# Gate biases, ln1's vectors and the residual x loaded on GpSimd's queue, and ten low weight parts made by adding DMAs

## The chip, the cores and the metric

The kernel runs on one core of a Trainium2 chip. The metric is the time of one execution on the device in microseconds (us). The engines are TensorE (PE in the profile), VectorE (DVE), ScalarE (ACT), GpSimd (POOL) and SyncE (SP). SP does no arithmetic here, it issues DMAs; GpSimd does arithmetic and issues DMAs from its own queue. Each engine, and each queue of DMA issues, takes its instructions strictly in order: one that waits holds up all behind it.

## The reference

One layer of an encoder on 512 tokens of 1024 channels, in float32. Only the parts that matter here:

```python
mod = silu(c) @ w_ada + b_ada                       # 6 vectors of 1024: shift, scale, gate for both halves
h = normalize(x) * (1 + sc_m) + sh_m
q, k, v, u, g_sb, g_ssm = split(h @ w_in)           # token mixer
y_sb  = stick_breaking_attention(q, k, v) @ w_sb_up # 8 heads of 64
y_ssm = s5_branch(u, ..., w_glu, b_glu) @ w_ssm_up
y = (sigmoid(g_sb) * y_sb + sigmoid(g_ssm) * y_ssm) @ w_out
x = layer_norm(ALPHA * x + (1 + g_m) * y, ln1_g, ln1_b)
h = normalize(x) * (1 + sc_f) + sh_f
gate, up = split(h @ w_ffn_in)                      # channel mixer, 2816 hidden
y = (silu(gate) * up) @ w_ffn_out
x = layer_norm(ALPHA * x + (1 + g_f) * y, ln2_g, ln2_b)
```

## The kernel before

Every float32 product is made of three products of a rounded type: operands are split into a high part (a cast) and a low part (the value less its high part), and `mm3` adds high by high, high by low and low by high. So each weight tile, 128 partitions of 1024 values (512 KB, `raw`), is loaded by SP, cast to `whi` on ScalarE, and its low part `wlo` is made in one of two ways: by a subtraction on VectorE or GpSimd (`sub`), or by a copy with factor -1 on ScalarE and a DMA from GpSimd's queue that adds `raw` to it (the adding DMA, L181; `unit` with no engine given). There are 8 buffers for `raw` (the w_ada tiles, `ra`, use the same ones) and 4 each for `whi` and `wlo`. All other tiles of 128 x 512 lie in 53 slots (`s`), given out first in, first out.

The stages in order of time: the normalisation and the S5 branch with the projections q, k, v (to 155 us); attention over four pairs of heads (155 to 324 us), between whose steps the products of 16 gate tiles (g_sb, g_ssm) stand; the glu and the up-projections (to 389 us); w_out in two halves of two token blocks, `proj` (389 to 440 us); the layer norm `ln1_block` for four token blocks (412 to 478 us); the channel mixer (478 to 808 us), and the last layer norm (to 823 us).

After each of the gate tiles 9 to 15, `later` puts a piece of the work on w_ada. The first four are `ada_gate`: GpSimd clears the tile (L257), a row of b_ada is loaded into its first partition by SP, two w_ada tiles are loaded by SP, and VectorE adds their 8 slices up, each times a value of c (L252). The tile that is cleared is a slot that an earlier product must have released.

The order of each engine's instructions is worked out ahead of time by a scheduler with streams of priorities ("feed" for weights, "attn", "gates", "later", "mix", "ffn"), from its own estimates of durations. Only SP's loads (`load`, L146) keep the order in which the program is written. ln1's gain and shift (`bcast`, four loads) stand in front of the glu weights in that order; the residual x of a token block is loaded in `proj` ahead of that half's w_out tiles, and GpSimd scales one half of it (L921).

In the channel mixer the first two pairs of column tiles (`first`) are two tiles through `unit` and two through `slot_unit`; FENG gives GpSimd the low parts of three and VectorE that of one. Both are needed when ln1's output h of two token blocks is there (`first_half(0)`). Behind it stand the products `p_x1` and `p_b` of further column pairs (dp = 0, 1 first), whose low parts VectorE makes in `operand`, then `first_half(256)`.

## Time and profile before

| | |
|---|---|
| median of 3 runs | 826.23 us (822.55 to 826.59) |
| the profiled execution | 824.6 us, its span 822.9 us |
| TensorE busy | 758.1 us (92%) |
| VectorE busy | 586.4 us (71%) |
| ScalarE busy | 438.8 us (53%) |
| GpSimd busy | 148.4 us (18%) |
| TensorE's mean granted clock | 0.968 of full speed |

A busy share is an average over stages. In 153 to 244, 340 to 440 and 520 to 804 us TensorE has no gap; its idle time lies in the first 60 us, in 244 to 331 us, in 440 to 478 us and at the end. In the profile the name of a buffer has no number: `s` is any slot, `b` a PSUM bank.

### The profile page before, as it was taken

How to read it: one execution, taken by the hardware profiler on the slowest of the kernel's cores; microseconds unless marked ns; L12 is line 12 of the kernel's file. 1: busy time of each engine (PE TensorE's matmuls, PEld its weight loads, DVE VectorE, ACT ScalarE, POOL GpSimd, SP SyncE). 2: the span in 40 equal slices, each digit the busy share in tenths (PEclk: the TensorE clock that was granted, in tenths of full speed). 3: DMA queues.
4: the chain of work that ended last, by engine and by line, in shares of the span. 5: the costliest groups of instructions: out<-in, count | busy, mean ns of one | idle time of the engine just before them, and what ended most of it. 6: DMA issues, size and time to landing. Idle time of an engine off the chain costs nothing.

```text
span 822.9 us, 12321 instructions
## 1 busy us (share of the span) xinstructions
PE 758.1 (92%) x4767; PEld 667.5 (81%) x4767; DVE 586.4 (71%) x975; ACT 438.8 (53%) x715; POOL 148.4 (18%) x161
## 2 busy tenths in 40 slices
PE   4989989999996797999994999999999999999995
PEld 2878879988885676787883989999999999888884
DVE  5798474884658774878799898777787876434267
ACT  4375644678987676761435473534445456532211
POOL 1443244512323221001634000000000000000013
PEclk9999998999997999899998899999999999999998
DMA  9992227964207792925941004414445344440001
GB/s 281 361 242 67 52 64 153 237 137 77 52 10 196 228 232 92 350 70 187 358 120 52 1 19 136 155 53 146 144 143 183 104 139 145 157 148 27 1 26 76
DMA packets 99498, 111.49 MB, mean 135 GB/s; under 512 B 4456, under 2 KB 86384, under 8 KB 99440
## 3 DMA queue, kind: packets, MB, share of 16 engines
q1 hardware_dynamic: 95552, 96.82, 37.1%
...
q14 instruction: 21, 0.17, 0.1%
...
## 4 chain that ended last, share of the span: by engine, by line
PE 75%; DVE 10%; DMA 6%; issue 3%; ACT 2%; SPq 2%; POOL 1%; POOLq 0%; DVEq 0%; ACTq 0%
PE b L149 74%; DMA ra<-w_ada 3%; SPq L146 2%; DMA s<-w_in 1%; DVE s L252 1%; DVE st L288 1%; DMA raw<-w_glu 1%; DMA wlo<-raw 1%; DVE h L159 1%; DVE s L407 1%; DMA s<-x 0%; DVE s L159 0%; DVE s L972 0%; DVE s L943 0%; DVE s L477 0%
## 5 line engine op out<-in xcount | busy, mean ns | idle before, releaser
L149 PE MATMUL b<-h,whi 128*128 128x256 f32 (+1 forms) x896 | 216.5, 331 | 20.8 <-DVE h L159 9.4
L149 PEld LDWEIGHTS b<-h,whi 128*128 128x128 f32 x896 | 151.5, 191 | 36.5 <-DVE h L159 9.6
L159 DVE TENSOR_TENSOR wlo<-raw,whi 128x1024 fp32r<-128x1024 f32 x103 | 129.6, 1264 | 72.1 <-ACT whi L178 37.1
L149 PE MATMUL b<-s,whi 128*128 128x256 f32 (+1 forms) x800 | 168.5, 308 | 7.6 <-ACT whi L178 6.8
L149 PE MATMUL b<-h,wlo 128*128 128x256 f32 (+1 forms) x448 | 148.2, 331 | 1.4 <-DMA wlo<-raw 1.4
L149 PEld LDWEIGHTS b<-s,whi 128*128 128x128 f32 x800 | 129.7, 190 | 18.0 <-ACT whi L178 6.9
L149 PE MATMUL b<-whi,s 128*128 128x512 f32 (+1 forms) x392 | 122.6, 390 | 0.0
L149 PE MATMUL b<-s,wlo 128*128 128x256 f32 (+1 forms) x400 | 121.5, 306 | 0.0
L159 DVE TENSOR_TENSOR s<-s,s 128x512 fp32r<-128x512 f32 (+4 forms) x112 | 76.4, 689 | 56.4 <-PE b L149 23.0
L178 ACT CAST whi<-raw 128x1024 fp32r<-128x1024 f32 x66 | 69.0, 1048 | 84.7 <-PE b L149 66.5
L1054 ACT CAST whi<-raw 128x1024 fp32r<-128x1024 f32 x70 | 72.7, 1050 | 77.5 <-PE b L149 41.6
L149 PEld LDWEIGHTS b<-h,wlo 128*128 128x128 f32 x448 | 85.8, 192 | 8.9 <-DMA wlo<-raw 1.9
L149 PEld LDWEIGHTS b<-whi,s 128*128 128x128 f32 x392 | 73.2, 188 | 16.6
L149 PE MATMUL b<-s,s 128*128 128x128 f32 (+2 forms) x438 | 81.9, 317 | 2.0 <-POOL s L159 1.4
L164 ACT CAST s<-s 128x512 fp32r<-128x512 f32 (+1 forms) x106 | 57.7, 569 | 41.3 <-DMA s<-w_in 12.1
L149 PEld LDWEIGHTS b<-s,wlo 128*128 128x128 f32 x400 | 75.7, 190 | 3.7
L149 PEld LDWEIGHTS b<-s,s 128*128 128x128 f32 x438 | 68.5, 192 | 11.2 <-POOL s L159 1.6
L149 PE MATMUL b<-wlo,s 128*128 128x512 f32 (+1 forms) x196 | 76.4, 390 | 0.0
L1233 POOL TENSOR_TENSOR s<-s,s 128x512 f32<-128x512 f32 x6 | 8.5, 1430 | 357.1 <-DVE s L1232 357.1
L159 POOL TENSOR_TENSOR s<-s,s 128x512 fp32r<-128x512 f32 (+1 forms) x32 | 40.2, 1264 | 79.0 <-ACT s L164 77.6
L1047 DVE TENSOR_TENSOR raw<-raw,raw 128x1024 f32<-128x1024 f32 x40 | 48.6, 1219 | 4.8 <-DMA raw<-w_ffn_in 4.3
L252 DVE SCALAR_TENSOR_TENSOR s<-ra,ca,s 128x256 f32<-128x256 f32 x88 | 47.2, 557 | 4.0 <-DMA ra<-w_ada 3.2
...
## 6 DMA issues: line engine op xcount, KB each, us to landing
...
```

Source lines behind the costliest of these rows:

```text
L146: return tc.keep_in_program_order(nc.sync.dma_start(out=o, in_=i))
L149: return nc.tensor.matmul(o, lhsT, rhs, start=start, stop=stop, skip_group_check=True, **kw)
L159: return eng.tensor_tensor(dst, a, b, ALU.subtract)
L164: acopy(h[:, :n], x[:, :n])
L178: acopy(hi, raw)
L252: stt(dst, r_, ca[:, k:k + 1], init if k == 0 else dst, ALU.mult, ALU.add)
L288: V.bn_stats(st[:, i, :], x)
L407: e.scalar_tensor_tensor(p_, n, -c, p_, ALU.mult, ALU.add)
L1047: tt(r, x, y, ALU.add)
L1054: acopy(hi, x)
L1233: G.tensor_tensor(z[h], z[h], l2b[h], ALU.add)
```

## The change

A new helper, `aside`, issues a load on GpSimd's queue, in whatever place the scheduler gives it. It takes the loads of the b_ada rows (eight), of ln1's and ln2's vectors (four each) and of the residual x (eight of 256 KB). In `proj` the x loads, and GpSimd's scaling of one half, are written behind the w_out tiles instead of ahead of them. A new helper, `lower`, makes a low part; with no engine given it does so by ScalarE's copy and an adding DMA. With it the four tiles of `first` (FENG is gone) and the operands of `p_x1` and `p_b` for dp = 0 and 1 get their low parts by ten adding DMAs (two of 128 x 1024 and four of 128 x 512, then four of 128 x 1024). In the changed file the lines move: L149 becomes L153, L159 becomes L163, L181 becomes L169, L257 becomes L264; `aside` is L150.

```diff
@@ -57,7 +57,7 @@
 PL = 5
 TAIL = 256
 
-ENG, FENG = "VGVVVGVGGGGVVGGG", "GGGV"
+ENG = "VGVVVGVGGGGVVGGG"
 
 
 XE, BE, ME, HE = "VVVV", "VVVV", "VVAVAAAV", "VVVVVVVV"
@@ -145,6 +145,10 @@
     def load(o, i):
         return tc.keep_in_program_order(nc.sync.dma_start(out=o, in_=i))
 
+    def aside(o, i):
+
+        return G.dma_start(out=o, in_=i)
+
     def mm(o, lhsT, rhs, start, stop, **kw):
         return nc.tensor.matmul(o, lhsT, rhs, start=start, stop=stop, skip_group_check=True, **kw)
 
@@ -158,17 +162,24 @@
     def sub(dst, a, b, eng=V):
         return eng.tensor_tensor(dst, a, b, ALU.subtract)
 
+    def lower(l, x, h, eng):
+
+        if eng is None:
+            act(l, x, AF.Copy, scale=-1.0)
+            G.dma_start(out=l, in_=x, accum_op=ALU.add)
+        else:
+            sub(l, x, h, eng)
+
     def split(x, n=512, eng=V, keep=False):
 
         h, l = get(F32R), get(F32R)
         acopy(h[:, :n], x[:, :n])
-        sub(l[:, :n], x[:, :n], h[:, :n], eng)
+        lower(l[:, :n], x[:, :n], h[:, :n], eng)
         if not keep:
             put(x)
         return h, l
 
     def unit(view, a, b, eng=V):
-
 
         with prio("feed"):
             raw = wp.tile([P, D], F32, tag="raw", name=nm("raw"), bufs=NRAW)
@@ -176,11 +187,7 @@
             hi = wp.tile([P, D], F32R, tag="whi", name=nm("whi"), bufs=NHI)
             lo = wp.tile([P, D], F32R, tag="wlo", name=nm("wlo"), bufs=NHI)
             acopy(hi, raw)
-            if eng is None:
-                act(lo, raw, AF.Copy, scale=-1.0)
-                G.dma_start(out=lo, in_=raw, accum_op=ALU.add)
-            else:
-                sub(lo, raw, hi, eng)
+            lower(lo, raw, hi, eng)
         return hi.rearrange("p (a b) -> p a b", a=a), lo.rearrange("p (a b) -> p a b", a=a)
 
     def slot_unit(view, a, b, eng=V):
@@ -255,14 +262,14 @@
 
         col = j * D + i * 256
         G.memset(dst, 0.0)
-        load(dst[0:1, :], I["b_ada"][0:1, col:col + 256])
+        aside(dst[0:1, :], I["b_ada"][0:1, col:col + 256])
         ada_acc(dst, w_ada[:, :, col:col + 256], 256, dst)
 
     def ada_gate_pe(j, i, dst):
 
         col = j * D + i * 256
         G.memset(dst, 0.0)
-        load(dst[0:1, :], I["b_ada"][0:1, col:col + 256])
+        aside(dst[0:1, :], I["b_ada"][0:1, col:col + 256])
         o = bk.get()
         for k0 in (0, 4):
             raw = wp.tile([P, D], F32, tag="raw", name=nm("ra"), bufs=NRAW).rearrange("p (k n) -> p k n", k=4)
@@ -276,7 +283,7 @@
         g = []
         for i in range(2):
             x_ = get()
-            load(x_, I[name][0:1, i * 512:(i + 1) * 512].partition_broadcast(P))
+            aside(x_, I[name][0:1, i * 512:(i + 1) * 512].partition_broadcast(P))
             g.append(x_)
         return g
 
@@ -913,12 +920,6 @@
         pre = exp_table(sig)
         def proj(blocks):
 
-            for i in blocks:
-                po[i] = [bk.get(), bk.get()]
-                xr[i] = [get(), get()]
-                for h in range(2):
-                    load(xr[i][h], I["x"][i * P:(i + 1) * P, h * 512:(h + 1) * 512])
-                G.tensor_scalar(xr[i][1], xr[i][1], ALPHA, None, ALU.mult)
             for k in range(KC):
                 view, eng = w_o[:, k:k + 1, :], (V, G)[ENG[k + 8 * (blocks[0] // 2)] == "G"]
                 if k >= KEEP:
@@ -926,6 +927,12 @@
                 elif k not in wo:
                     wo[k] = slot_unit(view, 1, D, eng)
                 later(("out", blocks[0] // 2 * 8 + k))
+            for i in blocks:
+                po[i] = [bk.get(), bk.get()]
+                xr[i] = [get(), get()]
+                for h in range(2):
+                    aside(xr[i][h], I["x"][i * P:(i + 1) * P, h * 512:(h + 1) * 512])
+                G.tensor_scalar(xr[i][1], xr[i][1], ALPHA, None, ALU.mult)
             cut = KC - CUT
             for ks, bs in [([k], blocks) for k in range(cut)] + [(range(cut, KC), [i]) for i in blocks]:
                 for i in bs:
@@ -1005,10 +1012,10 @@
             for c in (0, FH):
                 view = w_f[:, :, c + P * i:c + P * i + P]
                 if len(first) < 2:
-                    w = unit(view, KC, P, (V, G)[FENG[len(first)] == "G"])
+                    w = unit(view, KC, P, None)
                     w = [[x[:, k, :] for x in w] for k in range(KC)]
                 else:
-                    pair = slot_unit(view, KC, P, (V, G)[FENG[len(first)] == "G"])
+                    pair = slot_unit(view, KC, P, None)
                     wx += pair
                     w = [[x[:, k % 4 * P:k % 4 * P + P] for x in pair[k // 4]] for k in range(KC)]
                 first.append(w)
@@ -1047,16 +1054,16 @@
                 tt(r, x, y, ALU.add)
             return r
 
-        def operand(x):
+        def operand(x, eng=V):
             with prio("feed"):
                 hi = wp.tile([P, D], F32R, tag="whi", name=nm("whi"), bufs=NHI)
                 lo = wp.tile([P, D], F32R, tag="wlo", name=nm("wlo"), bufs=NHI)
                 acopy(hi, x)
-                sub(lo, x, hi)
+                lower(lo, x, hi, eng)
             return hi, lo
 
-        def product(o, x, h, first):
-            w = operand(x)
+        def product(o, x, h, first, eng=V):
+            w = operand(x, eng)
             for q in range(2):
                 for k in range(4):
                     cs = slice(k * 256 + q * P, k * 256 + q * P + P)
@@ -1104,14 +1111,14 @@
             d = dps[dp]
             d["a"], d["c"] = piece(dp, 0, 0), None
             d["X"], d["c1"] = bk.get(), get()
-            product(d["X"], d["a"], half(0, 0), True)
+            product(d["X"], d["a"], half(0, 0), True, None if dp < 2 else V)
             acopy(d["c1"], d["X"])
 
         def p_b(dp):
             d = dps[dp]
             d["b"] = piece(dp, 0, 4)
             o = bk.get()
-            product(o, d["b"], half(4, 0), True)
+            product(o, d["b"], half(4, 0), True, None if dp < 2 else V)
             tt(d["c1"], o, d["c1"], ALU.add)
             bk.put(o)
             silu(d["c1"])
```

The scheduler then orders the engines anew. GpSimd's queue where the gate biases are cleared, before the change (s29 is the tile for the first two pieces of the gate bias; wlo_448 and wlo_454 are low parts of the gate tiles 10 and 11):

```order
L159 TENSOR_TENSOR s48_369_2318<-s39_367_2315,s18_368_2317 128x384
L159 TENSOR_TENSOR s8_381_2375<-s37_379_2372,s3_380_2374 128x384
L159 TENSOR_TENSOR s34_378_2369<-s44_376_2366,s6_377_2368 128x512
L257 MEMSET s29_425_2638 128x256 x2
L181 DMA wlo_448_2747<-raw_446_2744 128x1024
L159 TENSOR_TENSOR s15_404_2502<-s14_402_2499,s24_403_2501 128x384
L159 TENSOR_TENSOR s36_413_2553<-s8_411_2550,s35_412_2552 128x512
L159 TENSOR_TENSOR s38_416_2559<-s41_414_2556,s0_415_2558 128x384
L181 DMA wlo_454_2794<-raw_452_2791 128x1024
```

And after it (wlo_490 is the low part of gate tile 12):

```order
L169 DMA wlo_454_2794<-raw_452_2791 128x1024
L163 TENSOR_TENSOR s48_369_2318<-s39_367_2315,s18_368_2317 128x384
L163 TENSOR_TENSOR s8_381_2375<-s37_379_2372,s3_380_2374 128x384
L169 DMA wlo_490_2962<-raw_488_2959 128x1024
L163 TENSOR_TENSOR s34_378_2369<-s44_376_2366,s6_377_2368 128x512
L264 MEMSET s29_425_2638 128x256 x2
L150 DMA s29_425_2638<-b_ada 1x16x16 x2
L163 TENSOR_TENSOR s15_404_2502<-s14_402_2499,s24_403_2501 128x384
```

The adding DMAs of three gate tiles, one of which directly followed the clearing before and two of which came later still, now stand ahead of it; the b_ada rows follow the clearing on the same queue.

TensorE's queue where the gates end, before the change (h0 with wlo_527 or whi_526 is gate tile 15, the last; `ident` rows turn the S5 outputs; b4 by s23 and s39 are the last head's products):

```order
L149 MATMUL b6_72<-h0_64,wlo_527_3191 128x512
L149 MATMUL b6_72<-h0_64,whi_526_3190 128x512
L149 MATMUL b6_72<-h1_65,whi_526_3190 128x512
L149 MATMUL b6_72<-h0_64,wlo_527_3191 128x512
L842 MATMUL b0_66<-ident_99,s26_163_998 128x128 x4
L842 MATMUL b1_67<-ident_99,s7_195_1181 128x128 x4
L842 MATMUL b2_68<-ident_99,s4_227_1364 128x128 x4
L842 MATMUL b3_69<-ident_99,s5_259_1547 128x128
L149 MATMUL b4_70<-s23_514_3123,s24_469_2863 128x256
L842 MATMUL b3_69<-ident_99,s5_259_1547 128x128 x3
L149 MATMUL b4_70<-s39_515_3124,s24_469_2863 128x256
```

And after it, where the same turns stand (negones by s22 are the last head's running sums):

```order
L153 MATMUL b4_70<-s22_512_3106,negones_659 128x512
L153 MATMUL b4_70<-s22_512_3106,negones_659 128x2x128
L153 MATMUL b5_71<-s22_512_3106,negones_659 128x128
L153 MATMUL b3_69<-s34_505_3072,s24_469_2863 128x256
L849 MATMUL b0_66<-ident_99,s26_163_998 128x128 x4
L153 MATMUL b3_69<-s8_506_3073,s24_469_2863 128x256
L153 MATMUL b3_69<-s34_505_3072,s24_469_2863 128x128
L153 MATMUL b3_69<-s8_506_3073,s24_469_2863 128x128
L849 MATMUL b1_67<-ident_99,s7_195_1181 128x128 x4
L849 MATMUL b2_68<-ident_99,s4_227_1364 128x128 x4
L153 MATMUL b4_70<-s23_514_3123,s24_469_2863 128x256
L153 MATMUL b4_70<-s39_515_3124,s24_469_2863 128x256
```

The gate tile's products, which stood between the last head's sums and the turns, have all gone further ahead; the sums and the turns now follow each other, and products of the up-projection (whi_572) come after.

GpSimd's queue at w_out, after the change (s7, s9, ... are the x tiles; s27 and s28 are the low parts of w_out's tile k = 1, wlo_647 and wlo_653 those of k = 5 and 7):

```order
L150 DMA s31_670_3973<-x 128x512
L150 DMA s16_657_3831<-x 128x512
L150 DMA s10_672_3978<-x 128x512
L150 DMA s38_671_3974<-x 128x512
L150 DMA s34_673_3979<-x 128x512
L163 TENSOR_TENSOR wlo_647_3810<-raw_645_3807,whi_646_3809 128x1024
L935 TENSOR_SCALAR s25_655_3826<-s25_655_3826 128x512
L163 TENSOR_TENSOR s27_629_3774<-raw_627_3771,s20_628_3773 128x512
L163 TENSOR_TENSOR wlo_653_3822<-raw_651_3819,whi_652_3821 128x1024
L935 TENSOR_SCALAR s16_657_3831<-s16_657_3831 128x512
L163 TENSOR_TENSOR s28_631_3778<-raw_627_3771,s44_630_3777 128x512
```

Before, the four x tiles of the first half were loaded by SP, and GpSimd's queue held two scalings and then the low parts of k = 1. Now eight x loads, two scalings and two of the larger subtractions stand around them.

## Rows read from the trace of the kernel before

**Rows 1.** The chain that ended last, share of the span by line.

```profile
PE b L149 74%; DMA ra<-w_ada 3%; SPq L146 2%; DMA s<-w_in 1%; DVE s L252 1%; DVE st L288 1%; DMA raw<-w_glu 1%; DMA wlo<-raw 1%; DVE h L159 1%; DVE s L407 1%; DMA s<-x 0%; DVE s L159 0%; DVE s L972 0%; DVE s L943 0%; DVE s L477 0%
```

**Rows 2.** Stages: length, busy of PE, PEld, DVE, ACT, POOL; PEclk, DMA, GB/s.

```profile
244.00:331.00 87.00, 67.77 (x331) 56.16 (x331) 58.75 (x114) 62.95 (x111) 20.70 (x22) 0.89 0.67 187
...
340.00:440.00 100.00, 100.00 (x451) 81.10 (x450) 85.14 (x135) 46.66 (x74) 29.44 (x14) 1.00 0.58 191
```

**Rows 3.** What SP's DMA queue waited for: us in total, times, longest us.

```profile
SPq L146 <- POOL s L257: 41.9, 2, 29.7
```

**Rows 4.** SP's issues: start us, us, engine line op out<-in xcount.

```profile
244.49 0.31 SPq L146 DMA_DIRECT2D s<-b_ada  x1
...
315.47 1.25 SPq L146 DMA_DIRECT2D s<-ln_g  x2
...
324.31 0.93 SPq L146 DMA_DIRECT2D raw<-w_glu  x2
```

**Rows 5.** TensorE, 236 to 331 us, [idle before <-releaser]: four of nine gaps.

```profile
254.71 0.73 PE L149 MATMUL b<-h,whi 128*128 128x512 f32 x2 [2.14 <-ACT whi L178]
...
260.60 0.80 PE L149 MATMUL b<-h,wlo 128*128 128x512 f32 x1 [1.02 <-DMA wlo<-raw]
...
288.25 0.99 PE L149 MATMUL b<-h,whi 128*128 128x512 f32 x2 [4.74 <-ACT s L706]
...
330.77 0.79 PE L149 MATMUL b<-s,whi 128*128 128x512 f32 x1 [6.78 <-ACT whi L178]
```

**Rows 6.** TensorE at the end of attention.

```profile
315.86 0.45 PE L149 MATMUL b<-h,wlo 128*128 128x512 f32 x1
...
321.05 1.58 PE L842 MATMUL b<-ident,s 128*128 128x128 f32 x13
...
322.84 1.16 PE L149 MATMUL b<-s,s 128*128 128x256 f32 x7
```

**Rows 7.** ScalarE at the end of attention.

```profile
316.06 0.98 ACT L767 ACTIVATE s<-b 128x512 f32<-128x512 f32 x2 [1.04 <-PE b L149]
...
321.85 3.82 ACT L844 COPY s<-b 128x512 f32<-128x512 f32 x4
```

**Rows 8.** Two stretches in attention, columns as in the stages.

```profile
256.00:272.00 16.00, 12.50 (x42) 9.67 (x43) 12.59 (x21) 10.49 (x21) 7.32 (x8) 0.68 0.36 71
...
288.00:300.00 12.00, 10.23 (x43) 8.48 (x44) 8.38 (x20) 7.64 (x15) 2.29 (x3) 0.86 1.10 287
```

**Rows 9.** The adding DMA: issue in ns, and landing in us.

```profile
L181 POOL DMA_DIRECT2D wlo<-raw x26: 827/869/1057, 50.9 to 303.6; - x26
...
DMA to landing us min/median/max: 4.5/5.2/8.9
```

**Rows 10.** GpSimd at w_out and at the end of ln1's first half.

```profile
380.83 1.50 POOL L921 TENSOR_SCALAR s<-s 128x512 f32<-128x512 f32 x1 [57.45 <-DVE s L252]
...
391.30 1.84 POOL L159 TENSOR_TENSOR s<-raw,s 128x512 fp32r<-128x512 f32 x1 [5.03 <-ACT s L164]
...
398.95 5.92 POOL L159 TENSOR_TENSOR wlo<-raw,whi 128x1024 fp32r<-128x1024 f32 x2
...
438.91 2.39 POOL L159 TENSOR_TENSOR wlo<-raw,whi 128x1024 fp32r<-128x1024 f32 x1 [0.55 <-ACT whi L178]
```

**Rows 11.** VectorE in the layer norm.

```profile
439.17 2.68 DVE L159 TENSOR_TENSOR h<-s,h 128x512 fp32r<-128x512 f32 x1
...
445.84 1.20 DVE L159 TENSOR_TENSOR wlo<-raw,whi 128x1024 fp32r<-128x1024 f32 x1
```

**Rows 12.** TensorE in and behind the layer norm.

```profile
454.32 0.58 PE L149 MATMUL b<-h,whi 128*128 128x256 f32 x1 [9.44 <-DVE h L159]
...
475.10 0.50 PE L149 MATMUL b<-h,whi 128*128 128x256 f32 x2 [0.64 <-ACT whi L1054]
```

**Rows 13.** The casts of the channel mixer's operands: busy us, mean ns.

```profile
L1054 ACT CAST whi<-raw 128x1024 fp32r<-128x1024 f32 x70 | 72.7, 1050 | 77.5 <-PE b L149 41.6
```

**Rows 14.** The gates' products by the high part, 244 to 331 us.

```profile
L149 PE MATMUL b<-h,whi 128*128 128x512 f32 x110 | 37.6, 419 | 6.9 <-ACT s L706 4.7 <-ACT whi L178 2.1
```

## The prediction

> **What bounds the kernel now.** I read the chain first, then the stages, then the gaps of TensorE in the stage that has most. The chain is TensorE for three quarters; the only other lines of weight are the landing of w_ada tiles (3%) and SP's queue (2%) [rows 1]. So the kernel is bound by TensorE's products, and time is to be had only where TensorE stands still or runs at the lower clock. From 340 to 440 us it has no gap at all [rows 2]; from 244 to 331 us it is busy for 67.8 of 87 us, so 19.2 us are idle [rows 2]. That stretch holds the last attention heads, the last gate tiles and the first pieces of w_ada.
>
> What holds it up there is seen in SP's queue. Its longest waits on GpSimd are two on the clearing of the gate bias tile, 41.9 us together, the longer 29.7 [rows 3]: the load of the b_ada row cannot go before the tile is cleared, the tile is cleared only when its slot is released, and all SP's later loads stand behind it. The first b_ada load leaves at 244.49 [rows 4]; the weights of gate tiles 10 to 15 and the w_ada tiles come behind it and the next in bunches, and the landing of w_ada is on the chain for 3% of the span, 25 us [rows 1]. TensorE pays in nine gaps. Four follow weights or what they hold up: 2.14, 1.02 and 4.74 us [rows 5] and a small one, 8.3 in all. The last is 6.78 us before the glu [rows 5], and four waits inside attention make the rest, 19.2 - 8.3 - 6.8 = 4.1. The glu waits because its weights leave SP only at 324.31: ln1's vectors (315.47 and later) wait in front of them for slots [rows 4].
>
> **The change part by part.** The terms are summed from the profiled execution, 824.6 us; the median of the runs shown lies 1.6 us above it.
>
> *b_ada and ln1 off SP's queue.* No load of a weight waits for a clearing or for ln1's slots any more; SP is limited by its eight buffers alone. Three casts and adding DMAs of gate weights move ahead of the clearing on GpSimd's queue, as the order shows. So the four weight gaps, 8.3 us, go. What is late next is attention itself. The three engines have much the same work in the stretch: TensorE 67.8, ScalarE 63.0, VectorE 58.8 us [rows 2]. When the gate products come earlier they no longer cover the last head. At present gate tile 15 runs from 315.86 until the turns at 321.05, 5.2 us, and the last head's products end at 324.0 (322.84 + 1.16) [rows 6]. ScalarE starts on that head's exponentials at 316.06, and its copies of the turns run from 321.85 to 325.7 [rows 7], so the first glu operand can be cast at about 326: a path of 10 us from the last head's sums to the glu. With the gate products gone TensorE has 3 us of turns and head products in it [rows 6], and by the changed order nine products of the up-projection, 2.1 us at 0.23 us each (5.2 us over gate 15's 22 to 23 products), so about 5 us stay idle instead of 6.8. Before that point the same head's earlier steps are uncovered too: between none and 6 us, by what its own ScalarE and VectorE steps take; I put 3. The tail is then 8 us, the attention waits stay at 4.1, together 12.1 against 19.2: 7.1 us gained. The bounds: all but the 5 us tail goes (14 gained), or the uncovered steps cost 6 and the attention waits double (0 gained).
>
> *The clock.* Two stretches behind these gaps were granted 0.68 over 12.5 busy us and 0.86 over 10.2 [rows 8], means between the two levels of 2.4 and 1.2 GHz. Against full speed that cost 0.32 x 12.5 + 0.14 x 10.2 = 5.4 us. The gaps of 2.14, 1.02 and 4.74 that precede the slow parts go, those of attention stay, so I take 4 of it back; from 0 to 5.4.
>
> *Loads on GpSimd's queue.* An issue there takes 0.83 to 1.06 us [rows 9]; the 24 loads cost GpSimd 21 us in all, and it is busy 20.7 of 87 us in the stretch and 29.4 of 100 at w_out [rows 2]. Two of ln1's issues, 1.7 us, stand ahead of the last head's weight subtractions; that is in the 3 us above. The issues at w_out are the next term. The b_ada rows land behind the clearing as before; only VectorE's sums wait for them, and the gate bias is used first behind the mixer.
>
> *x behind w_out.* Eight x loads stand ahead of GpSimd's subtractions for w_out's tile k = 1. They go as the up-projection's last products release their slots, 25 products of 0.23 us apart (5.8 us) by the order, while eight issues take 7.0 [rows 9], so 1.2 us are left behind the last release. Then come a subtraction of about 3.0 (5.92 for two), a scaling of 1.5 and k = 1's own 1.84 [rows 10]: 6.3 us, with the 1.2 in all 7.5. TensorE reaches k = 1 39 products, 9.1 us, behind that release. Of the 1.6 us to spare the scaling may need more, as it waits for its x to land, and the issues can be late: a stall of 0 to 3 us; I take 1. SP's own w_out loads come earlier without x in front.
>
> *First pair by adding DMAs.* In the layer norm VectorE loses four subtractions (two of 1.20 us as in [rows 11], and two of half the size, some 0.6): 3.6 us, of which I count 3.4, since each overlaps its neighbours a little. GpSimd's subtraction at 438.91 [rows 10] is gone as well; VectorE's own at 439.17 took 2.68 us beside it, where one of twice the size takes 1.20 [rows 11], so some 2 us of it are waiting. I count 1 of these, since ScalarE's cast ahead may be late next. TensorE's wait of 9.44 us for that path [rows 12] shortens by 4.4. The DMAs themselves are early, as their weights are loaded long before.
>
> *p_x1 and p_b.* Their low parts use the four wlo buffers, two of which stay with the first pair. p_b's two therefore wait until p_x1's two are read, 31 products of half the length, 0.12 us (3.7 us), ahead of use. Now a cast of 1.05 [rows 13] and a subtraction of 1.2 follow, and cost TensorE three small gaps, the first of 0.64 [rows 12], 1.8 us in all. After the change cast, copy, issue and landing follow: 1.05 + 1.05 + 0.87 + 5.2 [rows 9, 13] = 8.2, less 3.7 is 4.5 for the first and 0.3 for the second, 3.0 us more than now. The stretch behind the 4.74 us stop was granted 0.86 [rows 5, 8], which would cost 1.4 as there. So 4.4 comes back and 4.4 is given: 0, between 4 gained (landing 4.5 and no slow clock) and 5 lost (landing 8.9).
>
> The ten extra copies on ScalarE fall where it is busy 46.7 of 100 us [rows 2]; the rest of the channel mixer and the last layer norm are unchanged. Sum: 824.6 - 7.1 - 4 + 1 + 0 = 814.5, and with what the median lies above the profiled execution 816: I say 815 us.
>
> **A rule against it.** SP's queue stood for 41.9 us behind two clearings [rows 3]. The Trainium skill, "DMA: Bandwidth & Descriptors", section "Issuing engines are not separate DMA queues", says that issuing from several engines saves only the sequencer's time to issue, which is usually small. By it the gain would be the issues alone; the trace does not bear it out here, as the time was a wait in order and not an issue.
>
> **The rivals.** *Only issue time is saved (826).* Then the landing of w_ada at full DMA load (share 1.10 in 288 to 300 us [rows 8]) decides, and SP's removed issues of 0.3 to 1.3 us [rows 4] lie beside TensorE's work. Against it: in 256 to 272 us the DMA engines are at 0.36 [rows 8] while SP waits. *Attention is the bound (820).* The uncovered last head costs the 6 us of the bound above and attention's waits grow by 2: 12.1 + 5 = 17.1 us idle, 2 gained, with 3 from the clock, less 1 at w_out: 820.6. For it: ScalarE's 63 us [rows 2]. *Both ends good (805).* Gaps shrink to the 5 us tail, 14 gained, all 5.4 of the clock, and p_b gives back little. *Slower (832).* The gates' products run ahead of attention altogether, and it stands bare: the stretch holds 110 gate products by the high part [rows 14] and half as many by the low, 165 in all or 39 us, so attention's own are 67.8 - 39 - 5 (slow clock) = 24 us against some 48 us of ScalarE's work on it (63 less casts and copies of weights, 15). Each bare head of the last two would idle about 12 us, 24 to 27 in all against 19.2, 6 more; the slow clock behind them takes the place of today's 5.4 and the stall at w_out adds 1: 824.6 + 6 + 1, or 832 to 833 against the median. It decides if no gate product is left behind the start of the last pair. Against it: the order shows gate tiles 14 and 15 in between.
>
> **How the numbers follow.** Chances: the forecast 0.45 (from 809 to 819), both ends good 0.16, attention the bound 0.17, issue time only 0.10, slower 0.12. The range that leaves out a tenth on each side reaches from 804 to 828. A change of 0.5%, 4.1 us, is about what can be told from none: faster means under 822.1, slower over 830.4. Faster: 0.45 + 0.16 + most of the 0.17 = 0.75; the same: the rest of it and 0.10 = 0.14; slower 0.11.
>
> **What would show it.** In the profile after, SP's wait on the clearing is gone, and the gate and glu weights leave far ahead of their use; the 2.14, 1.02 and 4.74 us gaps are gone, and one stop of 4 to 8 us stands at the last head. At w_out TensorE waits for GpSimd's k = 1 by at most 3 us. In the layer norm the restart follows the end of w_out by some 4 us less, and p_b's first product waits about 4.5 us for an adding DMA. I am wrong if the stretch from 244 us to the glu does not shrink by at least 6 us, if several heads stand bare, or if the adding DMAs land late enough to eat what the gates gain.

## The result, and the profile after

The changed kernel takes **831.67 us** (median of five runs, 830.78 to 835.13) against 826.23 for the kernel before in the same session: a ratio of **1.0093, 95% interval 1.0067 to 1.0119**. The ratio, here and below, is not that of the two medians, which lie 5.4 us apart; gains are read from it, as it has the interval. By it the kernel is slower by some 7.7 us where the prediction had it 10 us faster; 831.67 lies outside the range of 804 to 828. A few executions of some kernels ran at a lower clock and took longer; the ratios leave them out, and as the profiled executions of e5 and e14 below were such, no distance in us is read from their traces, but for the lengths of VectorE's steps in e14. The profiled execution took 835.13 us (span 833.3), 3.5 us above the median, so single distances in its trace are read with that allowance.

First the stretch that the change was aimed at. SP's waits on the landing of adding DMAs, in the kernel before, in the kernel after, and in the kernel after from 425 to 460 us alone (us in total, times, longest us):

```profile
SPq L146 <- DMA wlo<-raw: 60.4, 10, 9.9
```

```profile
SPq L146 <- DMA wlo<-raw: 158.6, 23, 14.7
...
SPq L146 <- DMA wlo<-raw: 21.1, 2, 14.7
```

The wait on the clearing [rows 3] is gone; in its place SP waits for adding DMAs to land. Most of that is the gate tiles' own: with none of the ten new ones (e1 below) it is already 137.0 us, in 21 waits. TensorE in the kernel after, from 281 us to the start of the glu (six of its nine waits of 240 to 340 us):

```profile
282.12 0.56 PE L153 MATMUL b<-s,s 128*128 128x256 f32 x3 [1.69 <-DVE s L163]
288.45 0.81 PE L153 MATMUL b<-h,whi 128*128 128x512 f32 x2 [2.75 <-ACT s L713]
306.66 0.39 PE L153 MATMUL b<-s,s 128*128 128x256 f32 x1 [1.80 <-ACT s L176]
309.16 1.02 PE L153 MATMUL b<-s,s 128*128 128x256 f32 x4 [2.11 <-POOL s L163]
319.51 1.01 PE L849 MATMUL b<-ident,s 128*128 128x128 f32 x4 [1.95 <-ACT s L846]
325.39 0.74 PE L153 MATMUL b<-s,whi 128*128 128x512 f32 x2 [1.66 <-ACT s L851]
```

The gaps of 2.14 and 1.02 us [rows 5] are gone, that of 4.74 is 2.75, and the 6.78 before the glu is 1.66: the glu starts at 325.39 instead of 330.77. No gap here follows a weight any more; all follow attention's own steps on VectorE, ScalarE and GpSimd. The same stages as in [rows 2], and the two behind them (length, busy of PE, PEld, DVE, ACT, POOL; PEclk, DMA, GB/s):

```profile
244.00:326.00 82.00, 68.07 (x330) 57.46 (x329) 62.63 (x118) 58.69 (x105) 24.46 (x28) 0.92 0.63 174
340.00:440.00 100.00, 96.89 (x426) 78.26 (x424) 82.75 (x132) 47.26 (x75) 29.40 (x23) 0.97 0.53 166
440.00:478.00 38.00, 19.00 (x144) 18.71 (x145) 27.03 (x54) 21.22 (x48) 7.78 (x14) 0.73 0.43 90
478.00:500.00 22.00, 18.07 (x128) 17.20 (x127) 14.86 (x30) 15.20 (x29) 1.73 (x2) 0.84 0.25 49
```

So the 5.4 us gained by 325 us are lost behind it, mainly in two places, and the chain by line answers to [rows 1] with TensorE down from 74% and `wlo<-raw` second:

```profile
PE b L153 67%; DMA wlo<-raw 2%; DMA raw<-w_in 2%; DVE s L259 2%; SPq L146 2%; DVE s L163 1%; DMA s<-w_in 1%; DVE wlo L163 1%; DVE s L414 1%; DVE st L295 1%; DMA raw<-w_ssm_up 1%; ACT s L437 1%; DVE s L481 1%; DMA s<-x 0%; DVE s L380 0%
```

**At w_out**, where TensorE had no gap, it now has one, and 100 us are at 0.97 in place of 1.00. TensorE, VectorE and GpSimd of the kernel after there:

```profile
386.89 2.73 PE L153 MATMUL b<-ones,s 128*128 128x1 f32 x24
392.10 0.50 PE L153 MATMUL b<-ones,s 128*128 128x1 f32 x4
395.12 1.01 PE L153 MATMUL b<-ones,s 128*128 128x1 f32 x4 [2.52 <-DVE s L259]
...
383.42 3.10 DVE L259 SCALAR_TENSOR_TENSOR s<-ra,ca,s 128x256 f32<-128x256 f32 x1
387.04 0.47 DVE L259 SCALAR_TENSOR_TENSOR s<-ra,ca,s 128x256 f32<-128x256 f32 x1
391.48 2.84 DVE L163 TENSOR_TENSOR s<-s,s 128x512 fp32r<-128x512 f32 x1
...
383.81 2.41 POOL L163 TENSOR_TENSOR wlo<-raw,whi 128x1024 fp32r<-128x1024 f32 x1
391.24 2.54 POOL L163 TENSOR_TENSOR wlo<-raw,whi 128x1024 fp32r<-128x1024 f32 x1
```

The one-column products sum the w_ada slices over the partitions; they now stand in a bunch of 24, and the last of them waits for VectorE. Two of VectorE's steps beside GpSimd's subtractions take 3.10 and 2.84 us, where the first kind takes 0.47 a little later. Then the clock falls:

```profile
390.00:394.00 4.00, 2.60 (x14) 2.10 (x12) 4.00 (x3) 0.33 (x1) 4.00 (x4) 1.00 0.89 272
394.00:398.00 4.00, 2.88 (x9) 2.49 (x10) 2.86 (x5) 1.24 (x2) 4.00 (x3) 0.60 0.87 304
398.00:402.00 4.00, 4.00 (x12) 3.12 (x11) 0.00 (x0) 0.00 (x0) 2.27 (x2) 0.55 0.87 247
```

Against full speed (columns as in [rows 2]) that costs 0.40 x 2.88 + 0.45 x 4.00 = 3.0 us; with the stop of 2.5 it is 5.5 us.

**In ln1**, the restart came at 454.32 [rows 12], 13.5 us behind w_out's last product at 440.8. Now (TensorE, and the VectorE step that held it):

```profile
450.00 0.58 PE L153 MATMUL b<-h,whi 128*128 128x256 f32 x1 [10.58 <-ACT h L985]
459.79 0.58 PE L153 MATMUL b<-h,whi 128*128 128x256 f32 x1 [9.00 <-DVE h L163]
485.23 0.58 PE L153 MATMUL b<-h,wlo 128*128 128x256 f32 x1 [2.17 <-DMA wlo<-raw]
...
457.31 1.22 DVE L1054 TENSOR_TENSOR raw<-raw,raw 128x1024 f32<-128x1024 f32 x1 [9.30 <-DMA s<-b_ada]
458.45 1.28 DVE L163 TENSOR_TENSOR h<-s,h 128x512 fp32r<-128x512 f32 x2
```

w_out ends at 450.00 - 10.58 = 439.4, and the restart is 20.4 us behind it. VectorE stands 9.3 us at L1054, the sum of two raw weight tiles that `plus` makes for a later product, and the low parts of h that TensorE needs stand behind it. The row names a landing of b_ada as the last releaser; the sum itself reads only w_ffn_in tiles, and in other kernels below the same step waits for `raw<-w_ffn_in`. These come late because SP cannot issue them: a buffer of `raw` is free only when the adding DMA that reads it has landed (the 21.1 us from 425 to 460 above). The last of them, issued at 446.5, then took 10.5 us to land, among the adding DMAs; the median of such loads is 4.5. Of GpSimd's eight adding DMAs at this place, six for the first pair and two for operands of p_x1 and p_b, one stands at 406.79; the second and the last are, with the time to landing of all from 425 to 490 us:

```profile
433.47 0.90 POOL L169 DMA_DIRECT2D wlo<-raw  x1 [8.98 <-ACT wlo L168]
446.99 1.61 POOL L169 DMA_DIRECT2D s<-raw  x1
...
DMA to landing us min/median/max: 4.5/6.9/10.0
```

The wait ahead of that, 10.58 us where the kernel before had 3.56, has another cause: it ends with ScalarE's cast of h (L985). ScalarE, without a gap from 437.4 to 449.9, makes six copies for the adding DMAs (L168) ahead of it, 5.0 us. The copies and the cast in the kernel after, and the cast in the kernel before:

```profile
L168 ACT ACTIVATE wlo<-raw 128x1024 fp32r<-128x1024 f32 x3 | 3.2, 1052 | 0.0
L168 ACT ACTIVATE s<-raw 128x512 fp32r<-128x512 f32 x3 | 1.8, 613 | 0.0
...
449.33 0.61 ACT L985 CAST h<-s 128x512 fp32r<-128x512 f32 x1
...
443.71 0.62 ACT L978 CAST h<-s 128x512 fp32r<-128x512 f32 x1
```

The cast comes 9.9 us behind w_out's end instead of 2.9. For the restart at 459.79 the sum that VectorE waits for is later still: the casts of h are done at 449.9, the sum at 458.5.

### The profile page after: what moved, and what is told of

It reads as the page before. It is cut to its first block, busy times and chain, and to the rows that moved or that the text cites. A ratio compares the mean times of both kernels' runs of the same rounds, so it can differ in the third digit from the quotient of the medians.

```text
span 833.3 us, 12365 instructions
## 1 busy us (share of the span) xinstructions
PE 759.9 (91%) x4767; PEld 670.1 (80%) x4767; DVE 581.4 (70%) x969; ACT 446.9 (54%) x725; POOL 161.0 (19%) x191
## 4 chain that ended last, share of the span: by engine, by line
PE 67%; DVE 12%; DMA 7%; issue 6%; ACT 4%; SPq 2%; POOL 1%; POOLq 0%; DVEq 0%; ACTq 0%
PE b L153 67%; DMA wlo<-raw 2%; DMA raw<-w_in 2%; DVE s L259 2%; SPq L146 2%; DVE s L163 1%; DMA s<-w_in 1%; DVE wlo L163 1%; DVE s L414 1%; DVE st L295 1%; DMA raw<-w_ssm_up 1%; ACT s L437 1%; DVE s L481 1%; DMA s<-x 0%; DVE s L380 0%
## 5 line engine op out<-in xcount | busy, mean ns | idle before, releaser
L153 PE MATMUL b<-h,whi 128*128 128x256 f32 (+1 forms) x896 | 218.2, 333 | 23.5 <-ACT h L985 10.6
L153 PEld LDWEIGHTS b<-h,whi 128*128 128x128 f32 x896 | 152.5, 193 | 38.7 <-ACT h L985 10.8
L163 DVE TENSOR_TENSOR wlo<-raw,whi 128x1024 fp32r<-128x1024 f32 x99 | 120.4, 1222 | 69.6 <-ACT whi L189 39.9
L153 PE MATMUL b<-s,whi 128*128 128x256 f32 (+1 forms) x800 | 165.3, 305 | 1.7 <-ACT s L851 1.7
L153 PE MATMUL b<-h,wlo 128*128 128x256 f32 (+1 forms) x448 | 148.7, 332 | 2.2 <-DMA wlo<-raw 2.2
L153 PEld LDWEIGHTS b<-s,whi 128*128 128x128 f32 x800 | 128.1, 188 | 11.3 <-issue 2.1
L153 PE MATMUL b<-whi,s 128*128 128x512 f32 (+1 forms) x392 | 122.7, 390 | 0.0
L153 PE MATMUL b<-s,wlo 128*128 128x256 f32 (+1 forms) x400 | 120.8, 303 | 0.0
L163 DVE TENSOR_TENSOR s<-s,s 128x512 fp32r<-128x512 f32 (+4 forms) x112 | 83.1, 749 | 48.4 <-PE b L153 23.4
L153 PEld LDWEIGHTS b<-h,wlo 128*128 128x128 f32 x448 | 86.5, 193 | 9.3 <-DMA wlo<-raw 2.4
L153 PE MATMUL b<-s,s 128*128 128x128 f32 (+2 forms) x438 | 85.4, 325 | 7.0 <-ACT s L176 2.8
L153 PEld LDWEIGHTS b<-whi,s 128*128 128x128 f32 x392 | 73.1, 188 | 16.4
L153 PEld LDWEIGHTS b<-s,s 128*128 128x128 f32 x438 | 71.2, 197 | 17.2 <-ACT s L176 3.2
L153 PEld LDWEIGHTS b<-s,wlo 128*128 128x128 f32 x400 | 75.3, 188 | 3.5
L153 PE MATMUL b<-wlo,s 128*128 128x512 f32 (+1 forms) x196 | 76.3, 389 | 0.0
L1054 DVE TENSOR_TENSOR raw<-raw,raw 128x1024 f32<-128x1024 f32 x40 | 48.6, 1219 | 12.8 <-DMA s<-b_ada 9.3
L163 POOL TENSOR_TENSOR s<-s,s 128x512 fp32r<-128x512 f32 (+1 forms) x32 | 40.9, 1296 | 76.8 <-ACT s L176 62.3
L169 POOL DMA_DIRECT2D wlo<-raw x32 | 28.9, 903 | 128.0 <-ACT wlo L168 104.9
```

Source lines behind the costliest of these rows:

```text
L153: return nc.tensor.matmul(o, lhsT, rhs, start=start, stop=stop, skip_group_check=True, **kw)
L163: return eng.tensor_tensor(dst, a, b, ALU.subtract)
L169: G.dma_start(out=l, in_=x, accum_op=ALU.add)
L1054: tt(r, x, y, ALU.add)
```

## The experiments

Each time is a median, each ratio is to the kernel before on the same chip in the same session (its medians were 824.0 to 825.8). Percentages of differences are turned into us by 1% = 8.25 us. A difference of two such ratios is uncertain by about 2.5 us. Of e14 only the ratio is given.

### The parts apart

**e1: only b_ada and the vectors of ln1 and ln2 on GpSimd's queue**

```diff
-        load(dst[0:1, :], I["b_ada"][0:1, col:col + 256])
+        aside(dst[0:1, :], I["b_ada"][0:1, col:col + 256])
...
-            load(x_, I[name][0:1, i * 512:(i + 1) * 512].partition_broadcast(P))
+            aside(x_, I[name][0:1, i * 512:(i + 1) * 512].partition_broadcast(P))
```

> The kernel before with the b_ada rows and ln1's and ln2's vectors on GpSimd's queue, and nothing else of the change. Theory A (the whole change loses in the layer norm, because VectorE's sum of two weight tiles stands ahead of the last low parts of h and waits for buffers that adding DMAs release late): the loads alone keep what the gates gained, some 8 us, and TensorE restarts about 14 us behind the end of w_out as in the kernel before; 817 to 823 us. Rival B (it is GpSimd's queue, in which loads and adding DMAs stand in each other's way): no gain is left, 826 to 830. Rival C (gates that run ahead leave attention bare and w_ada's sums late): 826 or more, with the idle time between 300 and 400 us.

821.51 us, 0.9957 [0.994, 0.9975]: 3.5 us gained.

**e2: only the ten adding DMAs** (the kernel after with the two edits of e1 undone and x as in e4)

> The kernel before with the ten low parts by adding DMAs alone; b_ada, ln1's vectors and x are loaded by SP as before. Theory A: the wait of VectorE in the layer norm is there without any load on GpSimd's queue, and p_b's wait for an adding DMA too: 832 to 838 us. Rival B: without the loads in the same queue the adding DMAs are on time: 824 to 828. Rival C: 822 to 826, as the layer norm gains VectorE's four subtractions.

830.62 us, 1.0086 [1.0059, 1.0113], between theories A and B: they lose 7.1 us by themselves.

**e4: the kernel after with x on SP, ahead of w_out as before**

```diff
+            for i in blocks:
...
+                    load(xr[i][h], I["x"][i * P:(i + 1) * P, h * 512:(h + 1) * 512])
...
             for k in range(KC):
...
-            for i in blocks:
...
-                    aside(xr[i][h], I["x"][i * P:(i + 1) * P, h * 512:(h + 1) * 512])
```

> The changed kernel with x loaded by SP ahead of w_out as in the kernel before. Theory A: the layer norm's wait stays, at most the 2 to 3 us stop at 395 us goes: 829 to 833 us. Rival B: with eight loads less on its queue GpSimd is on time: 822 to 827. Rival C: 829 to 832, the stop at 395 us stays.

824.66 us, 1.0017 [0.9995, 1.0039], in rival B's range. Moving x alone is worth 0.76%, 6.3 us, of the loss.

**e7: e1 with x on GpSimd's queue behind w_out. e6: the kernel after with p_x1 and p_b on VectorE as before (so e7 with the first pair by adding DMAs). e9: e1 with the first pair by adding DMAs, x on SP ahead**

```diff
-            product(d["X"], d["a"], half(0, 0), True, None if dp < 2 else V)
+            product(d["X"], d["a"], half(0, 0), True)
...
-            product(o, d["b"], half(4, 0), True, None if dp < 2 else V)
+            product(o, d["b"], half(4, 0), True)
```

> The kernel of the first run (b_ada and ln1's and ln2's vectors on GpSimd's queue, no more adding DMAs) with x on GpSimd's queue behind w_out's tiles too. Theory A: x there costs 3 to 5 us by the stop at about 395 us, where TensorE waits for the sums on w_ada, as in the changed kernel: 824 to 827 us. Rival B (x costs only together with the adding DMAs): 820 to 822.

> The changed kernel with the low parts of the operands of p_x1 and p_b made by VectorE as before; the first pair's four tiles keep their adding DMAs. Theory A: p_b's wait of 2.2 us and the lower clock behind it go, and GpSimd's queue has four adding DMAs less when the first pair's are landing, so that the sum waits less: 823 to 827 us. Rival B (the first pair's adding DMAs alone make the wait in the layer norm): only p_b's 3 to 5 us go: 827 to 829.

> b_ada and ln1's and ln2's vectors on GpSimd's queue and the first pair's low parts by adding DMAs; x loaded by SP ahead of w_out and p_x1's and p_b's low parts by VectorE, both as before. Theory A, as it now stands (x behind w_out costs 6 to 7 us, p_b's adding DMAs 5, the first pair's gain 2): 818 to 821 us, faster than the first run's 821.5. Rival B (the first pair's adding DMAs make VectorE's sum wait, as in the second run): 823 to 826.

e7 828.72 us, 1.0049 [1.0029, 1.007], more than theory A had; e6 826.35, 1.0019 [0.9993, 1.0045]; e9 818.96, 0.9929 [0.9902, 0.9955]. The versions before, e1, e7, e6 and after differ by one part each, and so give each part its price on that way; the last column is the same part on another base:

| part | forecast | measured | on another base |
|---|---|---|---|
| b_ada, ln1 (e1 - before) | -11 | -3.5 | |
| x (e7 - e1) | +1 | +7.6 | +6.3 (after - e4) |
| first pair (e6 - e7) | -4.4 | -2.5 | -2.3 (e9 - e1) |
| p_x1, p_b (after - e6) | +4.4 | +6.1 | +7.3 (e4 - e9) |
| sum | -10 | +7.7 | |

A part's price depends on what is there already: the ten adding DMAs together cost 7.1 us on the kernel before (e2), 5.0 on e1 (e4 - e1) and 3.6 on e7 (after - e7). That is little more than such differences are uncertain by.

### What holds the layer norm up

**e3, e5 and e10: the first `plus` sum behind the low parts of h**, behind four of them in e3, behind all eight in e5 (both on the kernel after), and behind eight on e9 in e10 (`hlow` collects the subtractions that make these low parts)

```diff
-            s1 = plus(c_, d_)
+            with after(hlow[:8] if dp == 0 else []):
+                s1 = plus(c_, d_)
```

> The changed kernel, with the first sum of two weight tiles issued behind the low parts of h of the first two token blocks; all else is the same. Theory A: VectorE's 9.3 us wait no longer stands ahead of TensorE's restart; the restart comes 7 to 9 us sooner, and the time is 823 to 826 us. Rival B: the first pair's own low parts land no sooner, so TensorE waits for them: 829 to 832. Rival C: 830 to 832.

> The changed kernel with the first sum of two weight tiles issued behind the low parts of h of all four token blocks (the run before had it behind those of the first two, and VectorE then waited 6.2 us for it in front of the other two). Theory A (the sum waits for a weight load, the load for a buffer, the buffer for an adding DMA to land): VectorE has no wait of over 2 us between 440 and 475 us, TensorE restarts as in the run before and its gaps of 2.9 and 2.1 us before the turns of h go: 822 to 826 us. Rival B (the first pair's low parts and p_b's land late whatever VectorE does): 828 to 831.

> The run before with the first sum of two weight tiles behind the low parts of h of all four token blocks. Theory A: what is left of VectorE's wait in the layer norm goes, 816 to 819 us. Rival B (nothing waits there once x and p_b are as before): the same as the run before, within 1 us.

e3 829.08 us, 1.0055 [1.0035, 1.0076]; e5 827.80, 1.0025 [1.0001, 1.0049]; e10 **814.39, 0.9878 [0.9848, 0.9908]**. e3 came out in rival B's range, e5 just under that of its rival B, e10 under theory A's. So the order of one sum is worth 3.1 us (e3) and 5.6 (e5) on the kernel after, and 4.2 on e9. The restart's second wait of TensorE (at 454.32 [9.44] before) in e6, e9 and e10, with what VectorE waited for ahead of it in the first two:

```profile
452.32 0.58 PE L153 MATMUL b<-h,whi 128*128 128x256 f32 x1 [4.76 <-DVE h L163]
...
449.84 1.22 DVE L1054 TENSOR_TENSOR raw<-raw,raw 128x1024 f32<-128x1024 f32 x1 [1.55 <-DMA raw<-w_ffn_in]
```

```profile
447.56 0.58 PE L153 MATMUL b<-h,whi 128*128 128x256 f32 x1 [4.76 <-DVE h L163]
...
445.07 1.23 DVE L1054 TENSOR_TENSOR raw<-raw,raw 128x1024 f32<-128x1024 f32 x1 [2.01 <-DMA raw<-w_ffn_in]
```

```profile
442.86 0.58 PE L153 MATMUL b<-h,whi 128*128 128x256 f32 x1 [6.62 <-ACT h L986]
445.19 0.58 PE L153 MATMUL b<-h,whi 128*128 128x256 f32 x1 [1.53 <-DVE h L163]
```

With the sum out of the way the second wait is 1.53 us: what the first pair's adding DMAs free on VectorE only then reaches TensorE in full. e10 beats both kernels. The sum was not moved on e1 itself. There it stands ahead of the low parts of h too, but VectorE does not wait for it (445.88, 1.22 us, no idle time before it), so moving it should not bring the restart forward by more than these 1.2 us (an estimate from that row).

In e3, on the kernel after, TensorE has one wait in place of two:

```profile
448.22 0.58 PE L153 MATMUL b<-h,whi 128*128 128x256 f32 x1 [10.57 <-DVE h L163]
```

That is 9.0 us less than 10.58 + 9.00, but the sum then keeps VectorE waiting 6.15 us in front of the other low parts. And VectorE waits 1.26 us for ScalarE's cast of h ahead of this restart: with the sum gone, ScalarE's copies are what is late next.

### What x is worth, and how

**e8: e7 with x on SP, still behind w_out. e13: e7 with x on GpSimd's queue, but written ahead of w_out, where e4 has it.** The edit of e8:

```diff
-                    aside(xr[i][h], I["x"][i * P:(i + 1) * P, h * 512:(h + 1) * 512])
+                    load(xr[i][h], I["x"][i * P:(i + 1) * P, h * 512:(h + 1) * 512])
```

> As the run before, with x behind w_out's tiles but on SP's queue. Theory A (the cost is in the order: w_out's tiles come ahead of x and VectorE takes their low parts ahead of the sums on w_ada): the stop is there as on GpSimd's queue, 824 to 827 us. Rival B (the cost is GpSimd's queue: eight issues ahead of its low parts): 820 to 822.

> The kernel of the first run (b_ada and ln1's and ln2's vectors on GpSimd's queue) with x on GpSimd's queue too, but written ahead of w_out's tiles as before. Theory A (what matters is that SP no longer stands at x before w_out): w_out's tiles come as soon as with x behind them, 826 to 829 us. Rival B (what matters is where x is written): 820 to 823.

e8 827.16 us, 1.0028 [1.0005, 1.005]; e13 826.44, 1.0014 [0.9996, 1.0031]; both nearest to theory A. Neither the queue nor the place alone decides: all three versions lose 4.7 to 7.6 us against e1. What they share is that SP no longer stands at x before w_out. SP in e4 and in the kernel after:

```profile
370.51 5.34 SPq L146 DMA_DIRECT2D s<-x  x4
375.90 0.42 SPq L146 DMA_DIRECT2D raw<-w_out  x1
377.39 9.46 SPq L146 DMA_DIRECT2D raw<-w_out  x7
```

```profile
352.46 0.34 SPq L146 DMA_DIRECT2D raw<-w_out  x1
357.64 34.75 SPq L146 DMA_DIRECT2D raw<-w_out  x11
```

x needs slots that come free only late in the up-projection, so with x in front the weights of w_out were held back until 375; without it they come 23 us earlier, and the scheduler orders all three engines otherwise.

**e11, e12, e14 and e16: four attempts on the stop in the kernel after.** e11 puts the last four one-column products behind w_out's first half; e12 puts VectorE's low parts of w_out's first half behind the last merged operand; e14 makes GpSimd's k = 1, 5, 7 by adding DMAs; e16 spreads the 16 products among w_out's, by the edit shown with e17. The edits of e11, e12 and e14 (`done` collects w_out's products, `held_by` is the low part of the last merged operand, `hold` is empty outside w_out's first half; the lines that fill them are left out):

```diff
+            with after(done[-1:] if j >= 12 else []):
+                mm(ps[:, j:j + 1], sf_acc[j // 4][:, j % 4 * P:j % 4 * P + P], ones[:, 0:1], j == 0, True)
```

```diff
+            with after(hold if eng is V else []):
+                lows.append(sub(l, x, h, eng))
...
+            hold[:] = held_by if blocks[0] == 0 else []
```

```diff
-                view, eng = w_o[:, k:k + 1, :], (V, G)[ENG[k + 8 * (blocks[0] // 2)] == "G"]
+                view, eng = w_o[:, k:k + 1, :], None if blocks[0] == 0 and k in (1, 5, 7) else (V, G)[ENG[k + 8 * (blocks[0] // 2)] == "G"]
```

> The changed kernel with the last four of TensorE's products on the w_ada sums issued behind w_out's first half, where they stood at 417 us in the kernel before; x stays on GpSimd's queue behind w_out's tiles. Theory A (x costs because these products, in TensorE's order, wait for VectorE's last sum): the stop at 395 us and the lower clock behind it go, 826 to 829 us. Rival B (VectorE's low parts of w_out and of h come later by the new order, the stop is a symptom): 830 to 832.

> The changed kernel with VectorE's low parts of w_out's first half issued behind the last low part of the merged branches (where x, loaded by SP ahead of w_out, had kept them before). Theory A (x costs because w_out's tiles come some 20 us sooner and VectorE, full from 360 to 395 us, makes their low parts ahead of the merged operands that TensorE needs first): TensorE's 2.5 us stop at 395 us shrinks below 1 us or moves to the first low part of w_out, and w_out ends 3 to 5 us sooner: 826 to 829 us. Rival B (the x loads themselves, or GpSimd's work for w_out, are what is late): 830 to 833 us.

> The changed kernel with GpSimd's three low parts of w_out's first half (k = 1, 5, 7) by adding DMAs instead of its subtractions; VectorE's and all else as in the changed kernel. Theory A, in a new form (x off SP's queue brings w_out's tiles early, GpSimd's subtractions of them then run beside VectorE's last merged operands and w_ada sums, and stretch those from 0.5 to 2.6 us and more): no VectorE operation of 384 to 396 us takes over 1.3 us, the stop at 395 us goes, and w_out ends 3 to 5 us sooner: 826 to 829 us. Rival B (VectorE has too much to do there whatever GpSimd does, or the adding DMAs land as late): 830 to 834.

> The changed kernel with the 16 products on the w_ada sums (one column each, 24 of their 32 passes in one bunch of 2.7 us there) spread over w_out's first products, at most ten passes together. Theory A (what w_out's early tiles cost is TensorE's clock: the bunch of one-column products is followed by half clock for some 4 us, and the stop for the last sum comes on top): no half clock between 384 and 404 us and no stop at 395 us, 826 to 829 us. Rival B (the clock falls by the waits of VectorE and the bunch is chance): 830 to 833.

e11 832.30 us, 1.0092 [1.0057, 1.0128]; e12 834.77, 1.0125 [1.01, 1.0149]; e14 1.0128 [1.0092, 1.0165]; e16 834.54, 1.0126 [1.0104, 1.0147]. None helped, and none came into theory A's range. TensorE's stop in e11, e12 and e16:

```profile
396.53 5.71 PE L153 MATMUL b<-s,s 128*128 128x512 f32 x17 [2.74 <-ACT s L176]
```

```profile
394.58 7.68 PE L153 MATMUL b<-s,s 128*128 128x512 f32 x20 [3.89 <-DVE s L163]
```

```profile
397.76 0.50 PE L153 MATMUL b<-s,s 128*128 128x512 f32 x1 [4.26 <-ACT s L176]
```

What these products wait for in e11 (ScalarE, then VectorE):

```profile
395.86 0.62 ACT L176 CAST s<-raw 128x512 fp32r<-128x512 f32 x1 [4.04 <-DVE s L163]
...
392.99 2.84 DVE L163 TENSOR_TENSOR s<-s,s 128x512 fp32r<-128x512 f32 x1
```

The stop only moves to the next product in line, so in this version it is not the one-column products alone that are late. What ends it is a weight of w_out (`s<-raw`): in e11 and e16 ScalarE's cast, which stood 4.0 us until VectorE's low part of a merged operand was done (2.84 and 2.82 us, beside a subtraction of GpSimd), in e12 VectorE's low part, which the edit itself holds back. In e14 no step of VectorE from 380 to 410 us takes over 1.3 us, so the stretching is gone; the time is not better.

In e16, without the bunch, the clock still fell behind the stop: 0.59 from 398 to 402 us. On the kernel after's base the stop is enough for that.

**e15: e8 with GpSimd's k = 5 and 7 by adding DMAs, as in e14. e17: e15 with the one-column products spread** (`todo` lists the 16)

```diff
-                            mm3(po[i][h], [a[:, i * P:(i + 1) * P] for a in mg2[k]], wo[k][h], k == 0, k == KC - 1)
+                            r = mm3(po[i][h], [a[:, i * P:(i + 1) * P] for a in mg2[k]], wo[k][h], k == 0, k == KC - 1)
+                            if blocks[0] == 0 and todo:
+                                j = todo.pop(0)
+                                with after([r]):
+                                    mm(ps[:, j:j + 1], sf_acc[j // 4][:, j % 4 * P:j % 4 * P + P], ones[:, 0:1], j == 0, True)
```

> The kernel of the eighth run (loads on GpSimd's queue, x on SP behind w_out's tiles, no other adding DMAs) with GpSimd's two larger low parts of w_out's first half (k = 5, 7) by adding DMAs; no x load stands in GpSimd's queue here. Theory A (GpSimd's subtractions beside VectorE's merged operands and w_ada sums are what early tiles cost): no VectorE sum is stretched to 2.6 us, the stop at 395 us goes, 821 to 824 us. Rival B (early tiles cost in another way, such as the order in which w_out's token blocks end): 826 to 829 us.

> The run before last (loads on GpSimd's queue, x on SP behind w_out, k = 5 and 7 by adding DMAs) with the same spread. It had no stop at 395 us, but half clock from 394 to 398 us. Theory A: that stretch is at full clock, 2 us less: 823 to 825.5 us. Rival B: the stretch is still there, 826 to 828.

e15 826.91 us, 1.0025 [1.0003, 1.0047]; e17 822.46, 0.9975 [0.9962, 0.9988]. In e15 the stop of e8 (1.46 us) is gone, and the time is the same, in rival B's range; e17 is a little better than its theory A. The bunch is still there, and the stage behind it:

```profile
390.63 2.73 PE L153 MATMUL b<-ones,s 128*128 128x1 f32 x24
...
390.00:394.00 4.00, 4.00 (x31) 3.78 (x30) 3.04 (x5) 3.23 (x5) 2.98 (x3) 0.99 1.01 273
394.00:398.00 4.00, 4.00 (x14) 3.21 (x14) 3.31 (x3) 0.62 (x1) 3.79 (x3) 0.59 0.92 255
```

And the same stage in e17, where ten of them stand together:

```profile
390.99 1.17 PE L153 MATMUL b<-ones,s 128*128 128x1 f32 x10
...
390.00:394.00 4.00, 4.00 (x24) 3.46 (x24) 3.24 (x6) 3.36 (x6) 3.17 (x2) 1.00 1.00 278
394.00:398.00 4.00, 4.00 (x21) 3.13 (x20) 1.02 (x1) 0.19 (x1) 4.00 (x4) 1.00 0.76 222
```

TensorE is busy throughout in both; with the bunch it is granted 0.59, without it 1.00. That is 0.41 x 4.00 = 1.6 of the 4.1 us (0.50%) between the two. The order behind changes too: in the profiled runs w_out ends 1.0 us sooner in e17 (437.0 for 438.0) and the restart in ln1 comes 2.4 us sooner (453.66 for 456.05), so more of the gain stands in ln1 than in this stretch, and what makes it there was not followed. By the ratios e17 is within 0.18%, 1.5 us, of e1: with bunch and stop both gone nearly all of x's price is gone.

## Why the prediction was wrong

**x behind w_out: the step that failed.** The prediction priced it at +1 us, by GpSimd's issues pushing back k = 1. TensorE never waited for k = 1. It costs 6.3 us on e4 and 7.6 on e1, by something the prediction mentioned only as "SP's own w_out loads come earlier without x in front" and priced at nothing. In the kernel after, the visible part at w_out is the stop and the slow clock, 5.5 us: e4, equal to it up to 340 us (both 13.9 us idle from 240 us), ends w_out at 434.5, the kernel after at 439.4. A second part stands in ln1: SP's last w_ffn_in load of that time is issued at 438.1 in e4 and at 446.5 after, VectorE's wait at L1054 is 5.9 and 9.3 us, and the restart comes 13.9 and 20.4 us behind w_out's end. The two parts, 4.9 and 6.5 us, are those of profiled runs that lie 11.8 us apart, where the ratios give 6.3. On e1's base a part stands in ln1 too: the restart comes 13.5 us behind w_out's end in e1, 18.0 to 18.1 in e7, e8 and e15, and 16.7 in e17; why was not followed.

That the bunch of one-column products brings the clock down is shown on e15's base alone, by one pair of traces (e15 and e17). e7 agrees: with the same bunch the clock fell at 396.8, 0.6 us behind it and ahead of any stop. The kernel after and e8 do not: behind the same bunch they kept full clock for some 5 and 6 us and fell only after the stop had begun. So in the kernel after the slow clock is not shown to come from the bunch. The stop there can be followed to one step of VectorE, the low part of 2.84 us beside GpSimd's subtraction, but no run takes it away without making something else late: e11, e12 and e16 moved the stop, and e14 gained nothing. What it would be worth stays open.

VectorE's step of 0.47 us took 3.10 beside a subtraction of GpSimd. The Trainium skill, "SBUF — State Buffer", section "Who interferes with whom", says that a VectorE instruction with two inputs in SBUF contends with a GpSimd instruction that reads SBUF, that the ports they share are an exclusive lock, and that the order of issue decides who is blocked. The trace agrees that one waits for the other: VectorE's step ends 0.3 us behind GpSimd's (386.52 and 386.22); which of them asked first can't be told from their starts. But that is not what x costs by itself: in e8 two of these sums took 2.60 and 2.57 us, in e15 the longest there took 1.51, and the two kernels take the same time.

**Gates and ln1's vectors: right in kind, mis-sized by some 7.5 us.** Nearly all that was to show it did: the wait on the clearing gone, w_glu issued at 285.41 instead of 324.31, no gap behind a weight; of the 4.74 us, 2.75 are left. The idle time from 240 to 340 us was forecast at 12.1 and came to 12.9 in e1 and 13.9 in the kernel after, from 19.2. Only its form was wrong: not one tail of 4 to 8 us at the last head, but nine waits of 0.4 to 2.8 us in and behind attention. The clock was given back in part only: summed over the same stretch in pieces of 4 us, the slow clock cost 8.0 us before, 6.3 in e1 and 5.8 after; 4 were forecast to come back, about 2 did. That makes 6.4 + 1.7 = 8.1 us for e1 in the profiled runs to 340 us, against 11; at their end 5.7 of it are left (818.9 against 824.6), and by the ratio 3.5; e1's profiled run lies 2.6 below its median. Where the 2.4 between 8.1 and 5.7 went was not followed. "Only issue time is saved" is refuted by e1's interval, and so is the rule of the Trainium skill that was set against the step ("DMA: Bandwidth & Descriptors", "Issuing engines are not separate DMA queues"), as far as the end of a wait in order is concerned: the glu's stage starts 5.4 us sooner. That is under the 6 us that the prediction had set as a sign of being wrong; its other sign came too, as the ten adding DMAs cost 5.0 us on e1 (e4 - e1), more than the 3.5 gained. But it weighed less than the 41.9 us of waiting suggested.

**First pair: right mechanism, half the size.** -2.5 for -4.4. TensorE's two waits in ln1 are 3.59 and 9.14 us in e1, 6.64 and 4.76 in e9, 6.62 and 1.53 in e10: together 12.7, 11.4 and 8.2. So e10 has the 4.4 that were forecast, and e9 only 1.3 of it. The step that failed is "the DMAs themselves are early, as their weights are loaded long before". All but one are issued from 433.47 to 446.99, around w_out's end, and two of p_x1's and p_b's among them; while they last they hold `raw`, SP's next loads wait, and the `plus` sum that needs these loads stands ahead of the low parts of h on VectorE. e10 shows it: the sum moved, the gain is -0.79% against e1, 6.5 us, of which the sum's own 1.2 may be a part. "The ten extra copies on ScalarE fall where it is busy 46.7 of 100 us" was put at nothing and is wrong as to the place: six of them fall in ln1, where ScalarE has no gap for 12.5 us, and they lengthen the first wait. They do not set the restart, as long as the sum is later; in e3, with the sum moved, VectorE waits 1.26 us for ScalarE.

**p_x1 and p_b: right in sign, a little too small.** +6.1 and +7.3 for +4.4, about the uncertainty of such a difference. Half of the place was right: p_b's first product waits 2.17 us for its adding DMA (4.5 forecast) and 478 to 500 us has 0.84 (0.86 was taken). The other half is at ln1 again: the kernel after restarts 20.4 us behind w_out, e6 at 452.32, 14.1 us behind its end at 438.3, the first pair being the same in both; two more copies on ScalarE and two more adding DMAs stand there.

**The rivals.** The time of the "slower" rival came out (832), but not by its mechanism: attention did not stand bare, its stretch shrank. The prediction looked for the loss in the stretch that the loads leave and not behind it, where what they had held back arrives.
